# Entry and first layer of a two-layer fp32 backbone: clock products in a tile of their own, silu row copied in the last turn, two context dots from rows at hand, context projection behind the fourth conv

## The chip, the cores and the metric

The kernel runs on one core of one Trainium2 chip, as one launch. The metric is the device time in microseconds (us) of one execution; a result is the median of several runs. Five engines work side by side and wait for each other by semaphores: TensorE (PE: matmuls into PSUM), VectorE (DVE), ScalarE (ACT), GpSimd (POOL) and SyncE (SP), whose queue issues all loads here.

## The reference, cut to what matters

```python
def reference(x, c, ctx, c_ctx, ada_w, ada_b, ...):           # x (1,512,1024), ctx (1,256,1024), fp32
    for i in range(2):
        sh1, sc1, g1, sh2, sc2, g2 = ada(c, ada_w[i], ada_b[i])        # silu(c) @ ada_w + ada_b, in six parts
        csh1, csc1, ... = ada(c_ctx, ada_w[i], ada_b[i])
        h_l = rmsnorm(x, norm1_g[i]) * (1 + sc1) + sh1
        if i == 0:
            h_c = rmsnorm(ctx, norm1_g[i]) * (1 + csc1) + csh1
            p_lat, p_ctx = h_l @ w_in, h_c @ w_in                       # 384 q, 256 kv, 32 rotary key, 3 x 512 conv
            q, k, v = from rmsnorm(cq) @ w_uq, rmsnorm(ckv) @ w_ukv, norms and rotary   # latent and context
            a_l = softmax(q_l k_all^T) v_all                            # 8 heads, 512 queries, 768 keys
            b_gate, c_gate, u = split(p_lat[..., 672:], 3)
            s_l = b_gate * conv3(c_gate * u)                            # depthwise, width 3
            out_l = concat(a_l, s_l) @ w_o
        else:
            out_l = fourier(h_l) @ w_fourier
        x = x + g1 * out_l
        x = x + g2 * swiglu(rmsnorm(x, norm2_g[i]) * (1 + sc2) + sh2, ...)
    return x
```

The change lies in the first 150 us: the modulation of layer 0 (`ada`), the norm of x, the input projection of both streams and the conv.

## The kernel before

All activations are held transposed, with the 1024 features as eight tiles (k = 0..7) of 128 partitions, and the 512 latent or 256 context tokens along the row. Every operand of a matmul is split into a high and a low part (`h_hi`, `h_lo`, weights `...h`, `...l`), and `mm3` makes three matmuls of each product: high by high, high by low, low by high. A weight is loaded into one of six slots of the pool `rawp` (RAW = 6), cast by ScalarE into a high part and split by VectorE (`tensor_sub`, the name ending in `l`); high and low parts have three slots each, so a weight's cast waits until TensorE has finished with the weight three before. The rows of `ada_w` use the same six slots.

**Start.** ScalarE makes silu(c) and silu(c_ctx); TensorE spreads them over all partitions as rows, `sil0` in the PSUM tile cb0 (seen as `cb` in the trace) and `sil` in another, which ScalarE copies to `ccsil` at once. The row of silu(c) is wanted later in SBUF as `csil`, in two halves. VectorE, ScalarE and GpSimd square x, TensorE sums, VectorE makes the reciprocal root, and `first_rstd` transposes it into the first half of the PSUM tile `nxrb` (called `rb`). TensorE then runs `warm(WARM4, rb_tile)`, eight products of a matrix of ones (sixteen passes in the trace) whose result nobody reads and which keep its clock up; they are written to the second half of the same tile. ScalarE copies `rb` to SBUF as `rbs` for GpSimd; VectorE makes `xn` of the first tile, x times `rb`, straight from PSUM.

**The loop** goes over n = 0..7, k = ORDER[n] = 1, 2, 3, 4, 0, 5, 6, 7, with VectorE, ScalarE and TensorE in program order. `mod_dot(k, i)` is one VectorE instruction: a row of `ada_w` (128x1024) times `sil0` from PSUM, summed into one column of `mod` (the trace shows it as junk<-ada,cb with a DVE_READ_ACCUMULATOR behind it). In a turn ScalarE makes h_hi and nx of tile k, VectorE the first dot of the next tile, then h_lo of this one, then the second dot; ScalarE makes mod and amod from them and casts the next weight; TensorE takes 17 matmuls of the input projection into the tiles qkv0 to qkv2. GpSimd makes xn of the next tile. In turns 5 and 6 ScalarE also copies a half of `sil0` to `csil`.

**Behind the loop** the order is no longer written by hand: a scheduler places what the code names, instruction by instruction, so the order in the code sets priorities only. The code names two weight splits, the norms of cq and ckv, and then four calls of `conv(ct, side_work)`, each with three products of 24 matmuls: `ob`, `oc` and `ou`; after each product one more weight of the list `srcs` is loaded and split (`fetch`) and `side_work` is called. The side work of conv 0 and conv 1 is `ctx_work`: sixteen dots of rows of `ada_w` with `ccsil` (loads `adac`, written to `cmod`), the shift and scale of the context; then the context's norm (ncacc, ncst, ncrr, ncrb) and `norm_apply` (nct, hc_hi, hc_lo). `sq_q.mean` lets TensorE sum the squares of cq into `sqst`, which VectorE turns into `eps_q`; the slot of sqst is the one that `ob1` takes next. Between conv 2 and conv 3 stands the context projection `ckv` (69 matmuls), its norm (cc_hi, cc_lo, skcacc, skcst) and `rkv`. The side work of conv 2 and conv 3 is `g1w`, eight dots of the next modulation chunk with `csil`. Then follow `kpe` (the rotary key), four q tiles `qtok`, each with a rotary product on GpSimd that needs the table `rope_pack`, the k and v tiles and attention.

Of the kernel before, what the change touches and what calls it, by code (L numbers as in the profile page):

```python
# [58 lines left out]
WARM4 = 8  # L59
CTX_DOTS = 2  # L60
# [49 lines left out]
def backbone(ctx: ExitStack, tc: tile.TileContext, a, out):  # L110
    nc = Core(tc)
# [14 lines left out]
    def ps2(name):  # L126
        return ps["pool"].tile([P, 2, 512], F32, tag="s2", name=name, bufs=3)

    def ps1(name, bufs=2):
        return ps["pool"].tile([P, 512], F32, tag="b", name=name, bufs=bufs)  # L130
# [7 lines left out]
    def load(src, name, slots=None):  # L138
        t = slots(name) if slots else rawp.tile([P, src.shape[1]], F32, tag="raw", name=name)
        nc.sync.dma_start(out=t, in_=src)  # L140
        return t
# [22 lines left out]
    def step(it, n=1):  # L164
        for _ in range(n):
            next(it, None)
# [20 lines left out]
    cmod = const.tile([P, 16], F32, name="cmod")  # L187
# [11 lines left out]
    def dot(dst, w, vec):  # L199
        tc.keep_in_program_order(  # L200
            nc.vector.scalar_tensor_tensor(junk, w, 1.0, vec, op0=ALU.mult, op1=ALU.mult, accum_out=dst))
# [139 lines left out]
    def warm(n, on=None):  # L341

        o = (on or ps2("warm"))[:, 1]
        for i in range(n):
            nc.tensor.matmul(o[:, 0:P], ones, ones, start=True, stop=True)
# [4 lines left out]
    ccsil = p1.tile([P, D], F32, name="ccsil")  # L350
    warm(WARM)
    halves = [w.rearrange("p (two n) -> p two n", two=2) for w in (csil, ccsil)]
    sil0 = silu_rows(0)
    sil = silu_rows(1)
    warm(WARM2)
    rows = {}
# [62 lines left out]
    def first_rstd():  # L419

        st = ps2("nxst")[:, 0]
        sq = {}

        def square(k):
            sq[k] = early.tile([P, T], F32, tag="nsq", name=f"nxsq{k}", bufs=SQ_BUFS)
            xk = x[:, k, :]
            if k in SQ_DVE:
                nc.vector.tensor_mul(sq[k], xk, xk)
            elif k in SQ_POOL:
                tc.keep_in_program_order(nc.gpsimd.tensor_mul(sq[k], xk, xk))  # L430
            else:
                nc.scalar.activation(sq[k], xk, AF.Square)

        def col_sums(k, c):
            for t in range(4):
                nc.tensor.matmul(st[:, 4 * c + t:4 * c + t + 1], sq[k][:, t * P:(t + 1) * P], ones[:, 0:1], start=True, stop=True)

        for k in range(6):
            square(k)
            if k:  # L440
                nc.vector.tensor_add(sq[0], sq[0], sq[k])
        col_sums(0, 0)
        square(6)
        square(7)
        nc.vector.tensor_add(sq[7], sq[7], sq[6])
        col_sums(7, 1)
        mod_dot(order[0], 0)
        nc.scalar.copy(halves[1], sil)
        v, r = small("nxv", 4), small("nxr", 4)
        nc.vector.tensor_reduce(v, st[:, 0:8].rearrange("p (c t) -> p t c", c=2), op=ALU.add, axis=AX.X)  # L450
        nc.vector.tensor_scalar(v, v, 1.0 / D, EPS, op0=ALU.mult, op1=ALU.add)
        rsqrt(r, v, 4, "nxrs")
        rr = early.tile([P, 4, P], F32, name="nxrr")
        nc.vector.tensor_copy(rr, r.rearrange("p (t o) -> p t o", o=1).broadcast_to([P, 4, P]))
        o = ps2("nxrb")
        warm(WARM3, o)
        rb = o[:, 0]
        for t in range(4):
            nc.tensor.transpose(rb[:, t * P:(t + 1) * P], rr[:, t, :], ident)
        return rb, o  # L460

    order = ORDER
    mod_load(order[0])
# [2 lines left out]
    mod_load(order[1])  # L466
    mod_load(order[2])
    bias1 = p1.tile([P, KT], F32, name="bias1")
    rb, rb_tile = first_rstd()
    warm(WARM4, rb_tile)  # L470

    rbs = early.tile([P, T], F32, name="rbs")

    nc.vector.scalar_tensor_tensor(bias1, col(C_AB + 8, KT), 1.0, col(C_N1, KT), op0=ALU.add, op1=ALU.mult)
    mod_dot(order[0], 1)
    qkv_split(order[0])
    nc.scalar.copy(rbs, rb)
    nc.vector.tensor_mul(xn[:, order[0], :], x[:, order[0], :], rb)
    mod_finish(order[0])
    for fn in later:  # L480
# [7 lines left out]
    for n, k in enumerate(order):  # L488
        nxt, far, load_ = (order[n + i] if n + i < KT else None for i in (1, 2, 3))
        if load_ is not None:  # L490
            mod_load(load_)
        by_dve = nxt is not None and nxt >= NPE
        lo = hi_lo_affine(h_hi[:, k, :], h_lo[:, k, :], xn[:, k, :], amod0[:, k:k + 1], mod0[:, k:k + 1], T, f"nx{k}")
        if n in (5, 6):
            nc.scalar.copy(halves[0][:, n - 5], sil0[:, n - 5])
        if nxt is not None:
            tc.keep_in_program_order(nc.gpsimd.tensor_mul(xn[:, nxt, :], x[:, nxt, :], rbs))
        if by_dve:
            mod_dot(nxt, 0)
        lo()  # L500
        if n == 0 and XD == 2:
            nc.vector.tensor_mul(xn[:, nxt, :], x[:, nxt, :], rb)
        if by_dve:
            mod_dot(nxt, 1)
        if nxt is not None:
            mod_finish(nxt)
            qkv_split(nxt)
        by_pe = mod_pe(far) if far is not None and far < NPE else iter(())
        wh, wl = qw[k]
        r = (h_hi[:, k, :], h_lo[:, k, :])  # L510
        for i, (w, v) in enumerate(((wh, 0), (wl, 0), (wh, 1))):
            for m in range(5):
                nc.tensor.matmul((pq + pkv)[m], w[:, m * P:(m + 1) * P], r[v], start=(n == 0 and i == 0), stop=(n == 7 and i == 2))
                step(by_pe, 2)
            if i != 1:
                nc.tensor.matmul(ppe, wh[:, 640:704], r[v], start=(n == 0 and i == 0), stop=(n == 7 and i == 2))
# [18 lines left out]
        nc.vector.scalar_tensor_tensor(lo, src, g, f(hi), op0=ALU.mult, op1=ALU.subtract)  # L535

    srcs = [(f"wc{ct}_{w}", a["wconv"][ct, w]) for ct in range(3) for w in range(3)]
    srcs += [(f"wkvc{c}", a["wkvc"][c]) for c in range(3)]
    srcs += [(f"wc3_{w}", a["wconv"][3, w]) for w in range(3)]
    srcs += [(f"uq{k}", a["uq"][k]) for k in range(3)]  # L540
    stream, taken = [], []

# [70 lines left out]
    def ctx_work():  # L613
        for k in range(NPE, KT):
            for base in (0, 8):
                w = load(a["ada"][0, base + k], f"adac{base + k}")
                dot(cmod[:, base + k:base + k + 1], w, ccsil)
                yield
            nc.vector.tensor_add(pair_cols(cmod, k), pair_cols(cmod, k), pair_cols(cols[:, C_AB:C_AB + 16], k))
        scale_cols(camod, cmod[:, 8:16], col(C_N1, 8))  # L620
        rc = s_.rstd(0, L)
        yield
        norm_apply(p1, ctxT, rc, camod, cmod, hc_hi, hc_lo, 0, L, "nc")
        yield

    cw = ctx_work()
    conv(0, lambda: step(cw, CTX_DOTS))
    sq_q.mean(0, T, QL, eps_q)
    nc.vector.tensor_scalar_mul(eps_q, eps_q, EPS)
    conv(1, lambda: step(cw, CTX_DOTS))  # L630
# [2 lines left out]
    g1w = ada_chunk(0, 2)  # L633
    conv(2, lambda: step(g1w, 1))

    two, one_ = ps2("ckv01"), ps1("ckv2")
    ckv = [two[:, 0, 0:L], two[:, 1, 0:L], one_[0:ROPE, 0:L]]
    for c in range(3):
        w = weight()
# [10 lines left out]
    nc.scalar.copy(pe_f[0:32, T:T + L], ckv[2])  # L650
    sc_.mean(0, L, KVL, mkv[:, 4:6])
    rsqrt(rkv, mkv, 6, "rkv")
    conv(3, lambda: step(g1w, 2))
    step(g1w, 100)
    cv.release()
    p1.release()
# [780 lines left out]
    for t in range(4):  # L1437
        if t < 2:
            first(v1_ps[t], t, (3,))
            o = v1_ps[t]  # L1440
# [265 lines left out]
```

## Time and profile before

| | us |
|---|---|
| median of three runs | 1109.05 (1105.81 to 1110.4) |
| the profiled execution | 1111.21 |
| its span (first to last instruction) | 1109.4 |
| PE busy | 1072.6 (97%) |
| DVE busy | 862.5 (78%) |
| ACT busy | 533.0 (48%) |
| POOL busy | 134.1 (12%) |
| chain that ended last, by engine | PE 79%, DVE 11%, ACT 2%, issue 2%, DMA 1% |

The mean granted clock of TensorE is 0.983 of full speed. A busy TensorE is not TensorE at its peak, since matmuls are pipelined and their ends are modelled. In a row of a timeline the bracket gives the engine's idle time just before the instruction and what released it; a release can be a DMA that landed. Nearly every instruction has line L92, since a helper records it, so one goes by the names of tiles; the names leave out buffer numbers (`wc_0l` is the low part of the first weight of any of the four convs, `ob` the first product of any).

### The profile page before, as it was taken

To read this page: it belongs to the slowest core of one execution; us is meant where nothing else is said; L and a number is where in the kernel's file an instruction comes from. 1 tells how busy PE (TensorE), PEld (TensorE's weight loads), DVE (VectorE), ACT (ScalarE), POOL (GpSimd) and SP (SyncE) were. 2 spreads that over 40 slices of the span, in tenths; PEclk is the share of its full clock that TensorE was granted. 3 is DMA by queue.
4 is the path that set the end of the run, shared out by engine and by line. 5 is a ranking of instruction groups with operands and counts; after the bars stand their busy time and mean duration, and the time that the engine had idled before them with its cause. 6 is when DMAs were issued, how large, how long until landed. Compare 5 with 4: busy or idle time off the path is not lost.

```text
span 1109.4 us, 17136 instructions
## 1 busy us (share of the span) xinstructions
PE 1072.6 (97%) x6704; PEld 953.5 (86%) x6704; DVE 862.5 (78%) x1266; ACT 533.0 (48%) x842; POOL 134.1 (12%) x160
## 2 busy tenths in 40 slices
PE   8988998999999999999999999999999999999998
PEld 7667886888888898899989988987878899978997
DVE  5688868998789887889688989788895578745862
ACT  4553446898445452256415554363543155623550
POOL 1701138775000000000000000011000000000000
PEclk8998998999999999999999999898999999999999
DMA  7888540010661358643573573312425124431231
GB/s 251 289 300 267 171 154 24 23 56 27 223 226 58 120 183 267 208 152 117 188 230 132 172 256 134 95 58 82 147 72 163 51 88 140 134 96 67 76 95 67
DMA packets 45529, 156.96 MB, mean 141 GB/s; under 512 B 5252, under 2 KB 6276, under 8 KB 45320
## 3 DMA queue, kind: packets, MB, share of 16 engines
q1 hardware_dynamic: 45448, 155.87, 42.6%
q8 instruction: 52, 0.85, 0.3%
q14 instruction: 29, 0.24, 0.1%
HBM read 153.75 MB, written 2.10 MB: 140 GB/s over the span
## 4 chain that ended last, share of the span: by engine, by line
PE 79%; DVE 11%; ACT 2%; issue 2%; DMA 1%; POOL 0%; ACTq 0%; DVEq 0%; POOLq 0%
PE f L92 23%; PE s_a L92 13%; PE s_e L92 9%; PE s_f L92 4%; PE s_b L92 4%; PE s_ps L92 4%; PE o L92 3%; PE t_ps L92 2%; PE pv_ps L92 2%; PE ob L92 2%; PE z L92 2%; PE fo L92 2%; PE ou L92 2%; PE f_third L92 1%; DVE junk L92 1%
## 5 line engine op out<-in xcount | busy, mean ns | idle before, releaser
L92 DVE SCALAR_TENSOR_TENSOR junk<-ada,csil 128x1024 bf16<-128x1024 f32 x72 | 88.5, 1229 | 13.0 <-DMA ada<-in_ada 12.5
L92 DVE SCALAR_TENSOR_TENSOR x<-f,mod,x 128x512 f32<-128x512 f32 (+1 forms) x50 | 36.4, 728 | 66.1 <-PE f L92 66.0
L92 DVE TENSOR_TENSOR wu<-wu,wu 128x1024 f32<-128x1024 f32 x68 | 83.1, 1222 | 1.2
L92 POOL TENSOR_TENSOR w<-w,mod 128x1024 f32<-128x1024 f32 x4 | 7.9, 1974 | 478.0 <-DVE w_0l L92 460.1
L92 PE MATMUL s_a<-sh,w_s2h 128*128 128x256 f32 x136 | 38.5, 283 | 2.4 <-ACT s_b L92 2.4
L92 PE MATMUL s_a<-sh,w_s2l 128*128 128x256 f32 x136 | 38.5, 283 | 0.0
L92 PE MATMUL s_e<-sh,w_s1l 128*128 128x256 f32 x136 | 38.5, 283 | 0.0
L92 PE MATMUL s_e<-sh,w_s1h 128*128 128x256 f32 x136 | 38.3, 282 | 0.0
L92 PE MATMUL s_e<-sl,w_s1h 128*128 128x256 f32 x136 | 38.3, 282 | 0.0
L92 PE MATMUL s_a<-sh,w_s3l 128*128 128x256 f32 x136 | 38.3, 282 | 0.0
L92 PE MATMUL s_a<-sh,w_s3h 128*128 128x256 f32 x136 | 38.3, 282 | 0.0
L92 PE MATMUL s_a<-sl,w_s3h 128*128 128x256 f32 x136 | 38.2, 281 | 0.0
L92 PE MATMUL s_a<-sl,w_s2h 128*128 128x256 f32 x136 | 38.2, 281 | 0.0
L92 ACT CAST w_11h<-wu 128x1024 fp32r<-128x1024 f32 x17 | 17.8, 1049 | 41.1 <-PE f L92 18.0
L92 ACT CAST w_s2h<-wu 128x1024 fp32r<-128x1024 f32 x17 | 17.8, 1049 | 38.3 <-DVE wu L92 25.6
L92 DVE TENSOR_TENSOR w_22l<-wu,w_22h 128x1024 fp32r<-128x1024 f32 x17 | 20.8, 1225 | 19.2 <-ACT w_22h L92 19.2
L92 DVE TENSOR_TENSOR ptl<-t_ps,pth 128x384 fp32r<-128x384 f32 x62 | 31.4, 548 | 3.1 <-ACT pth L92 2.8
L92 POOL TENSOR_SCALAR p<-p,m 128x768 f32<-128x768 f32 x32 | 29.1, 910 | 25.1 <-DVE m L92 21.4
L92 DVE TENSOR_REDUCE m<-s_ps 128x1 f32<-128x768 f32 x32 | 30.3, 948 | 0.6 <-PE s_ps L92 0.5
L92 ACT CAST w_s1h<-wu 128x1024 fp32r<-128x1024 f32 x17 | 17.9, 1052 | 26.3 <-PE f L92 13.7
L92 ACT ACTIVATE p<-s_ps,m 128x768 f32<-128x768 f32 x32 | 29.2, 913 | 0.8 <-DVE m L92 0.8
L92 ACT CAST pth<-t_ps 128x384 fp32r<-128x384 f32 x62 | 26.7, 480 | 5.5 <-PE t_ps L92 5.1
(1016 smaller groups left out, 4174.5 us busy)
## 6 DMA issues: line engine op xcount, KB each, us to landing
ada<-in_ada SPq DMA_DIRECT2D x96, 512.0 KB, 4.4
wu<-in_wu SPq DMA_DIRECT2D x68, 512.0 KB, 3.8
w<-in_w SPq DMA_DIRECT2D x52, 512.0 KB, 4.2
adac<-in_ada SPq DMA_DIRECT2D x16, 512.0 KB, 4.8
wc<-in_wconv SPq DMA_DIRECT2D x12, 512.0 KB, 4.5
w<-in_w SPq DMA_DIRECT2D x16, 384.0 KB, 3.7
wo<-in_wo SPq DMA_DIRECT2D x8, 512.0 KB, 4.2
wf<-in_wf SPq DMA_DIRECT2D x8, 512.0 KB, 4.4
```

Of the source, the lines that this page charges most:

```text
L92: ins = fn(*args, **kw)
```

## The change

1. The clock products behind the transposes go to a tile of their own, `warm`, in place of the second half of `nxrb`.
2. ScalarE's copy `rbs` moves from before the first xn to behind h_hi and nx of turn 0.
3. Both halves of `csil` are copied in turn 7, in place of one each in turns 5 and 6.
4. In turn 7 VectorE makes the two context dots of tile 7 from the rows of `ada_w` that that turn's modulation has used (`rows[7]`), and `ctx_work` leaves tile 7 out: fourteen loads `adac` in place of sixteen.
5. Conv 0 steps the context dots once per weight in place of twice.
6. conv 3 is named before the context projection, and its weights before those of the projection in `srcs`.

```diff
         o = ps2("nxrb")
         warm(WARM3, o)
-        rb = o[:, 0]
+        rb = o[:, 0, :]
         for t in range(4):
             nc.tensor.transpose(rb[:, t * P:(t + 1) * P], rr[:, t, :], ident)
-        return rb, o
+        return rb
...
-    rb, rb_tile = first_rstd()
-    warm(WARM4, rb_tile)
+    rb = first_rstd()
+    warm(WARM4)
...
     qkv_split(order[0])
-    nc.scalar.copy(rbs, rb)
     nc.vector.tensor_mul(xn[:, order[0], :], x[:, order[0], :], rb)
...
-        if n in (5, 6):
-            nc.scalar.copy(halves[0][:, n - 5], sil0[:, n - 5])
+        if n == 0:
+            nc.scalar.copy(rbs, rb)
+        if n == 7:
+            for i in range(2):
+                nc.scalar.copy(halves[0][:, i], sil0[:, i])
...
         lo()
+        if n == 7:
+            for i, base in enumerate((0, 8)):
+                dot(cmod[:, base + k:base + k + 1], rows[k][i], ccsil)
...
     srcs = [(f"wc{ct}_{w}", a["wconv"][ct, w]) for ct in range(3) for w in range(3)]
+    srcs += [(f"wc3_{w}", a["wconv"][3, w]) for w in range(3)]
     srcs += [(f"wkvc{c}", a["wkvc"][c]) for c in range(3)]
-    srcs += [(f"wc3_{w}", a["wconv"][3, w]) for w in range(3)]
     srcs += [(f"uq{k}", a["uq"][k]) for k in range(3)]
...
             for base in (0, 8):
-                w = load(a["ada"][0, base + k], f"adac{base + k}")
-                dot(cmod[:, base + k:base + k + 1], w, ccsil)
-                yield
+                if k != order[7]:
+                    w = load(a["ada"][0, base + k], f"adac{base + k}")
+                    dot(cmod[:, base + k:base + k + 1], w, ccsil)
+                    yield
...
-    conv(0, lambda: step(cw, CTX_DOTS))
+    conv(0, lambda: step(cw, 1))
...
+    conv(3, lambda: step(g1w, 2))
     two, one_ = ps2("ckv01"), ps1("ckv2")
...
     rsqrt(rkv, mkv, 6, "rkv")
-    conv(3, lambda: step(g1w, 2))
     step(g1w, 100)
```

`warm` without a second argument takes a tile of the pool of pairs of PSUM banks, of which there are three; `warm` writes to its second half.

ScalarE at the start of the loop, before (wqkvh1 is the first weight's high part, nx1 and h_hi belong to turn 0):

```order
CAST wqkvh1_225<-wqkv1_143 128x672
COPY rbs_222<-nxrb_206 128x512
ACTIVATE mod_77<-mod_77,cols_68 128x1
ACTIVATE amod_79<-mod_77,bias1_159,cols_68 128x1
ACTIVATE h_hi_94<-xn_99,mod_77,amod_79 128x512
ACTIVATE nx1_243<-xn_99,mod_77,amod_79 128x512
```

and after:

```order
CAST wqkvh1_226<-wqkv1_143 128x672
ACTIVATE mod_77<-mod_77,cols_68 128x1
ACTIVATE amod_79<-mod_77,bias1_159,cols_68 128x1
ACTIVATE h_hi_94<-xn_99,mod_77,amod_79 128x512
ACTIVATE nx1_243<-xn_99,mod_77,amod_79 128x512
COPY rbs_223<-nxrb_206 128x512
```

The copy rbs stands four instructions later, behind the two that make turn 0's operand.

VectorE before eps_q, which releases ob1 (wc1_0l and wc1_1l are splits of conv 1's weights, a row with cmod_78<-adac is a context dot), before:

```order
TENSOR_TENSOR wc1_0l_657<-wc1_0_654,wc1_0h_656 128x1024
SCALAR_TENSOR_TENSOR junk_70,cmod_78<-adac3_758,ccsil_104 128x1024
SCALAR_TENSOR_TENSOR junk_70,cmod_78<-adac11_761,ccsil_104 128x1024
TENSOR_TENSOR cmod_78<-cmod_78,cols_68 128x2
TENSOR_TENSOR wc1_1l_696<-wc1_1_693,wc1_1h_695 128x1024
SCALAR_TENSOR_TENSOR junk_70,cmod_78<-adac4_795,ccsil_104 128x1024
SCALAR_TENSOR_TENSOR junk_70,cmod_78<-adac12_798,ccsil_104 128x1024
TENSOR_TENSOR cmod_78<-cmod_78,cols_68 128x2
TENSOR_SCALAR eps_q_518<-sqst0_717 128x4
```

and after:

```order
TENSOR_TENSOR wc1_0l_657<-wc1_0_654,wc1_0h_656 128x1024
SCALAR_TENSOR_TENSOR junk_70,cmod_78<-adac8_660,ccsil_104 128x1024
TENSOR_TENSOR cmod_78<-cmod_78,cols_68 128x2
SCALAR_TENSOR_TENSOR junk_70,cmod_78<-adac1_696,ccsil_104 128x1024
TENSOR_TENSOR wc1_1l_692<-wc1_1_689,wc1_1h_691 128x1024
TENSOR_SCALAR eps_q_521<-sqst0_710 128x4
```

Ahead of wc1_0l stood six context dots, and one does now; so ten dots of conv 0's and conv 1's work stood before eps_q, and three stand there now.

VectorE before wc2_2l, the low part that ou2 needs (z, y and mix are the conv's elementwise steps, ncv0 and ncrs0s belong to the context's norm), before:

```order
TENSOR_TENSOR wc2_1l_830<-wc2_1_827,wc2_1h_829 128x1024
TENSOR_TENSOR mix_84<-ob0_593,y0_710 128x512
TENSOR_TENSOR cmod_78<-cmod_78,cols_68 128x2
SCALAR_TENSOR_TENSOR camod_80<-cmod_78,cols_68 128x8
TENSOR_TENSOR z1_840<-ou1_725,cs1_801 128x512
TENSOR_SCALAR mkv_519<-skvst0_851 128x4
TENSOR_TENSOR wc2_2l_953<-wc2_2_950,wc2_2h_952 128x1024
```

and after:

```order
SCALAR_TENSOR_TENSOR junk_70,cmod_78<-adac12_850,ccsil_104 128x1024
SCALAR_TENSOR_TENSOR y1_837<-z1_833,cols_68,y1_837 128x512
TENSOR_TENSOR cmod_78<-cmod_78,cols_68 128x2
SCALAR_TENSOR_TENSOR junk_70,cmod_78<-adac5_854,ccsil_104 128x1024
TENSOR_TENSOR mix_84<-ob1_719,y1_837 128x512
SCALAR_TENSOR_TENSOR junk_70,cmod_78<-adac13_857,ccsil_104 128x1024
TENSOR_SCALAR ncv0_870<-ncst0_871 128x2
TENSOR_TENSOR cmod_78<-cmod_78,cols_68 128x2
SCALAR_TENSOR_TENSOR junk_70,cmod_78<-adac6_861,ccsil_104 128x1024
RECIPROCAL ncrs0s_876<-ncrs0s_876 128x2
TENSOR_TENSOR wc2_2l_950<-wc2_2_947,wc2_2h_949 128x1024
```

Before, all context dots were done ahead of wc2_1l; now they run up to wc2_2l, and one more (adac14) stands behind it.

## Rows read from the trace of the kernel before

**Rows 1.** Timeline of PE, 14 to 24 us: start, duration, instruction, [idle, releaser]

```profile
16.86 1.11 PE L92 MATMUL nxrb<-ident,nxrr 128*128 128x128 f32 x4 [1.19 <-DVE nxrr L92]
17.77 2.84 PE L92 MATMUL nxrb<-ones 128*128 128x128 f32 x16
22.91 1.55 PE L92 MATMUL qkv<-h_hi,wqkvh 128*128 128x512 f32 x3 [2.30 <-ACT h_hi L92]
```

**Rows 2.** The timeline of DVE, 14 to 34 us

```profile
17.94 0.08 DVE L92 DVE_READ_ACCUMULATOR junk<-ada,cb 128x1 f32 x1
21.26 0.69 DVE L92 TENSOR_TENSOR xn<-x,nxrb 128x512 f32<-128x512 f32 x1 [3.24 <-ACT rbs L92]
```

**Rows 3.** The timeline of DVE, 40 to 62 us

```profile
41.98 0.80 DVE L92 TENSOR_TENSOR h_lo<-nx,h_hi 128x512 fp32r<-128x512 f32 x1 [1.26 <-ACT nx L92]
...
46.91 1.22 DVE L92 SCALAR_TENSOR_TENSOR junk<-ada,cb 128x1024 bf16<-128x1024 f32 x1 [2.99 <-ACT csil L92]
...
48.06 0.69 DVE L92 TENSOR_TENSOR h_lo<-nx,h_hi 128x512 fp32r<-128x512 f32 x1
...
54.03 0.69 DVE L92 TENSOR_TENSOR h_lo<-nx,h_hi 128x512 fp32r<-128x512 f32 x1
...
58.38 0.78 DVE L92 TENSOR_TENSOR h_lo<-nx,h_hi 128x512 fp32r<-128x512 f32 x1 [2.52 <-ACT nx L92]
```

**Rows 4.** The timeline of PE, 60 to 96 us

```profile
62.17 0.39 PE L92 MATMUL ob<-h_hi,wc_0h 128*128 128x512 f32 x1
...
68.78 0.50 PE L92 MATMUL oc<-h_hi,wc_1h 128*128 128x512 f32 x1 [0.85 <-ACT skvacc L92]
...
80.08 0.95 PE L92 MATMUL sqst<-ones,sqacc 128*128 128x1 f32 x8
...
86.59 0.80 PE L92 MATMUL ob<-h_hi,wc_0h 128*128 128x512 f32 x1 [4.98 <-DVE eps_q L92]
...
94.42 0.40 PE L92 MATMUL oc<-h_hi,wc_1l 128*128 128x512 f32 x1
```

**Rows 5.** Windows: stretch, length, five engines, granted clock, DMA share, rate

```profile
87.00:95.00 8.00, 8.00 (x27) 6.31 (x27) 6.28 (x13) 1.86 (x4) 0.00 (x0) 0.73 0.89 299
95.00:105.00 10.00, 10.00 (x45) 7.97 (x43) 8.62 (x16) 4.52 (x8) 2.23 (x3) 1.00 0.92 311
```

**Rows 6.** The timeline of DVE, 80 to 106 us

```profile
85.04 1.22 DVE L92 SCALAR_TENSOR_TENSOR junk<-adac,ccsil 128x1024 bf16<-128x1024 f32 x1 [0.71 <-DMA adac<-in_ada]
...
86.39 0.15 DVE L92 TENSOR_SCALAR eps_q<-sqst 128x4 f32<-128x4 f32 x1
...
88.72 1.23 DVE L92 SCALAR_TENSOR_TENSOR junk<-adac,ccsil 128x1024 bf16<-128x1024 f32 x1 [1.97 <-DMA adac<-in_ada]
...
89.87 0.42 DVE L92 TENSOR_TENSOR ncacc<-ncacc,ncsq 128x256 f32<-128x256 f32 x1
90.20 1.22 DVE L92 TENSOR_TENSOR wc_2l<-wc,wc_2h 128x1024 fp32r<-128x1024 f32 x1
91.34 0.42 DVE L92 TENSOR_TENSOR ncacc<-ncacc,ncsq 128x256 f32<-128x256 f32 x1
...
104.31 0.69 DVE L92 TENSOR_TENSOR mix<-ob,y 128x512 f32<-128x512 f32 x1 [1.19 <-POOL z L92]
```

**Rows 7.** Chain of waits, 110 to 160 us: start, duration, group

```profile
112.74 5.60 PE ob L92 x24
...
123.71 8.15 PE ckv L92 x69
...
149.92 1.45 PE kpe_ps L92 x12
151.37 3.36 PE qtok L92 x18
...
156.55 0.40 DVE kr L92 x2
```

**Rows 8.** The page's DMA issues: group, KB each, us to landing

```profile
adac<-in_ada SPq DMA_DIRECT2D x16, 512.0 KB, 4.8
```

## The prediction

> **What bounds the kernel now.** TensorE is busy for 97% of the span, so the useful question is where it waits, and whether the edits touch those places. I read the instruction timeline of TensorE first, for the waits in brackets, then VectorE's timeline at the same times, to see what the releaser had been doing, then the granted clock by window, and last the chain of waits, for what carries a shift on to attention. In the first 62 us TensorE follows VectorE: the first projection matmul comes at 22.91 after 2.30 us of waiting for h_hi [rows 1], because VectorE's xn stood until 21.26, 3.24 us idle behind ScalarE's copy rbs [rows 2]. That copy reads the tile nxrb, into whose second half TensorE writes sixteen clock products from 17.77 to 20.61 [rows 1]. Then the loop is paced by VectorE and ScalarE: an undisturbed turn from h_lo to h_lo takes 4.35 us (54.03 to 58.38), but two turns take 6.08 and 5.97 us, each with a 2.99 us wait of a dot for ScalarE's csil copy [rows 3] (there are two such waits). From 62.17 TensorE is ahead and waits twice: 0.85 us before oc0, and 4.98 us before ob1, for eps_q [rows 4]. VectorE got to eps_q only at 86.39, since ten context dots and two weight splits stood in front of it, some late for their DMA [rows 6] (the dot at 85.04 is one of three such waits). After that gap the granted clock of the window 87 to 95 is 0.73 where the next has 1.00 [rows 5].
>
> **The change part by part.** *Clock products in their own tile.* xn now waits for the transposes alone, which end at 16.86 + 1.11 = 17.97; the dot before it is read out at 18.02 [rows 1, 2]. So xn starts at about 18.1 in place of 21.26: 3.2 us. The rbs copy, now behind h_hi and nx, ends near 18.1 + 4 x 0.69 = 20.9 (each step about as long as xn [rows 2]), so GpSimd, which waits for it, starts its first xn about as before, and that one is needed only a turn later; TensorE finishes the clock products at 20.6 and can start the projection at once. The loop is a chain through VectorE, so all 3.2 us carry to its end. Bounds: nothing (TensorE could be the later one if its first group runs at half rate), and 3.2; I take 3.2, since the wait behind an undisturbed turn is ScalarE's nx, not TensorE [rows 3], as at 58.38.
> The Trainium skill, page "PSUM — Partial Sum Buffer", section "PSUM bank collisions raise a hardware error", says that engines may use different banks side by side and clash only within one bank. The clock products already lay in another half of the tile, yet the copy waited for them [rows 1, 2], so the measurement says that here the wait goes by the whole tile. By the page too a separate tile leaves nothing to wait for, and the sum is the same.
>
> *csil copied in turn 7.* Without the copy the two dots of turns 5 and 6 start when VectorE is free, and both turns fall to the 4.35 us of the last: 6.08 + 5.97 - 2 x 4.35 = 3.35, of which I count 3.2, since most other turns are nearer 4.4. The copies now stand on ScalarE ahead of the cast of wc0_0, which has room. So the loop ends 6.4 us earlier and ob0, at 62.17 before, could start at 55.8.
>
> *Two context dots in turn 7, two loads dropped.* They cost VectorE 2 x 1.25 us right after h_lo, ahead of the split of wc0_0, whose result ob0's third matmul needs: 58.38 - 6.4 + 0.7 + 2.5 + 1.14 = 56.3, against 55.8 + 2 x 0.23 = 56.3. I put 0.2 us; the bound is 0 to 1. Two fewer loads of 512 KB relieve a busy queue and are counted at nothing.
>
> *Fewer dots in conv 0.* Before eps_q there were ten dots on VectorE, now there are three: 7 x 1.15 = 8.1 us less [rows 6], 88.72 to 89.87, and the three waits for loads go too. eps_q was late by 86.39 - 81.03, the end of sqst, = 5.4 us, so it is in time, and the gap before ob1 falls from 4.98 to some 0.2 us: 4.8 us. The wait before oc0 goes too (oc0 now takes the slot of qkv0, whose last reader on ScalarE is an earlier square than skvacc): 0.85. Without the gap, ob1 should run at full rate: it took 86.59 to 94.42, 7.83 us, where a conv product takes 5.60 [rows 4, 7]: 2.2 us.
>
> *Where those dots go.* Ten dots now stand between eps_q and the split of wc2_2, which ou2's third matmul needs. VectorE's work there, start to start from [rows 6]: ten dots at 1.15, four splits at 1.14, seven ncacc at 0.33, six 512-wide steps at 0.69 each, less their overlap (3.7 counted of 4.1), eight small ones (0.7): 22.8 us; plus 1.8 us in which the cast of wc2_0 waits for the end of ob1, and 1.2 for GpSimd's add before mix0, as at 104.31. That is 25.8 us. TensorE has ob1, 22 matmuls of oc1, ou1 and oc2 at 0.233 each (5.60, 5.13, 5.60, 5.60 [rows 7]), two column sums (0.8 and 0.5, from sqst's 0.95 [rows 4]), 0.2 for eps_q itself and two matmuls of ou2, 0.5: 23.9 us to the same point. So a **new wait of 1.9 us** in ou2, and 0.5 more at ncrb, whose norm stands behind two dots of the next chunk. Loss 2.4; bounds 0 (the loads early and the small steps hidden) and 5 (each of the last dots a little late).
>
> *Conv 3 ahead of the context projection.* The same matmuls in another order: ckv's 8.15 us and kpe's 1.45 us are paid in both [rows 7]. ob3 needs a slot freed by nct7: VectorE has fourteen steps of 256 columns before it (0.42 each, as ncacc), two splits and a dot, 9.3 us, TensorE has ob2 and twenty matmuls of oc3, 5.60 + 4.67 = 10.3 us: no wait. At the new border qtok0 needs uq2, whose slot ckv frees only at its end; its cast, 0.8, and split, 0.9 (three quarters of 1.14), with two short steps of ScalarE ahead, take some 2.4 us, and qtok0 has twelve matmuls first, two thirds of 3.36, 2.2 us [rows 7]. I take 0, bounds 0 to 1. kpe and skcst now run behind qtok0. The kr steps, which release GpSimd's rope and so the q and k chain up to attention, started 156.55 - 131.86 - 3 x 5.60 = 7.9 us behind the end of ckv, conv 3 left out; now they stand behind qtok0, two matmuls more, skcst and kpe, 3.4 + 0.3 + 0.6 + 1.45, and a copy of 0.3: 6.1, and five small steps of rkv, some 0.5, come among them. That is 1.3 us sooner. I count 0.5, because the rope load, which starts at the end of ckv as before, now has no conv 3 to cover it (on SP it also stands behind three row loads, and its products on GpSimd behind the add of conv 3); bounds -1.3 (gain) and +1.5 (kr waits for it).
>
> **Sum** against the profiled execution: -3.2 - 3.2 + 0.2 - 0.85 - 4.8 - 2.2 + 2.4 - 0.5 = -12.2 us. Its own time is 1111.2 us, which is 2.2 above the median of the three runs, 1109.05; so the changed kernel's profile should be near 1099.0 and its median near **1097 us**. What follows attention's start keeps its order and is bound by TensorE, so the shift should reach the end whole.
>
> **The rivals.** (1) *The clock falls at the new wait.* The 4.98 us gap was followed by slow matmuls [rows 5]; after the 0.85 us wait the 48 matmuls of oc0 and ou0 took 68.78 to 80.08, 0.235 each, full rate [rows 4]. 1.9 us lies between, and no row decides. It costs the same 2.2 us again: 1099.
> [...]
> (2) *The new tile doesn't free xn*: some other reader still holds it behind the clock products. Then 3.2 us stay: 1100. Against it: xn's only wait on TensorE is for the transposes. (3) *The border ckv to qtok0 loses instead of gaining*, by 2 to 3 us through uq2, skcst or the rope load: 1100. (4) *The moved dots wait for their loads.* This is the slower side. The ten dots behind eps_q share six load slots with weights that wait for TensorE. Before, one such dot stood 1.97 us for its DMA [rows 6]. If each of the ten did, ou2 would start 19.7 us later still: 1097 + 19.7 = 1117, slower. A mean of 0.65 us per dot brings it within 0.5%, and from 1.8 us it is slower by more. Against it: a load takes 4.8 us to land [rows 8], and by the new order each of these is issued when the third or fourth dot before it frees a slot, an estimated 5 us or more ahead; for it, that those three waits were there at all.
>
> **How the numbers follow.** Forecast as summed: 0.66, 1093 to 1100. Rival 1: 0.12; rival 2: 0.05; rival 3: 0.05; rival 4 in part (1104 to 1114): 0.08; in full: 0.04. A measurement of this kernel tells about 0.5% (5.5 us) from no change, so faster means below 1103.5. Faster is then the first four less a little for their tails, 0.87; same 0.09; slower 0.04. For 8 in 10 the range takes in rivals 1 to 3 and the unknown costs: no new wait gives 1094.5, with the border's whole 1.3 and csil's whole 3.35 1093.5, and the runs of the kernel before lie as far as 3.2 below their median, 1090; a new wait of 5 us with the clock's 2.2 gives 1102, and the border's worst 1104 to 1105. So 1090 to 1105.
>
> **What would show it.** Right: xn on VectorE near 18.1, no dot waiting for csil, h_lo of turn 7 near 52, ob0 near 56, ob1 right behind sqst near 74 with granted clock 1.00 between 75 and 95, a wait of about 2 us in ou2 near 98 for wc2_2l, ckv ending near 137, kr near 143. Wrong: xn still near 21; waits of VectorE for adac loads of a microsecond each between 75 and 100; a clock below 0.9 between 97 and 107; a gap between ckv and qtok1 above 1 us; or a shift at attention's start that the end doesn't keep.

## The result and the profile after

| us | before | after |
|---|---|---|
| median of four runs each, taken side by side | 1108.09 (1105.81 to 1110.4) | 1096.15 (1093.93 to 1097.64) |
| the profiled execution | 1111.21 | 1096.96 |
| its span | 1109.4 | 1095.2 |
| PE, DVE, ACT, POOL busy | 1072.6, 862.5, 533.0, 134.1 | 1066.9, 859.2, 533.3, 132.9 |

The ratio is 0.9891, with a 95% interval of 0.9862 to 0.9919: the changed kernel is 11.9 us faster. A second set of runs gave 1094.18 (six runs) against 1106.55 (eleven), ratio 0.9885 (0.9866 to 0.9904). Nearly the same work is done in both. PE is busy 5.7 us less, which fits the mean granted clock (0.983 before, 0.988 after), and the rest of the 14.2 us between the two spans is waiting.

The rows of the changed kernel follow in the order of rows 1 to 7. First TensorE's timeline from 14 to 24 us (start, duration, instruction, idle time before it and its releaser), which answers to [rows 1]:

```profile
17.22 1.11 PE L92 MATMUL nxrb<-ident,nxrr 128*128 128x128 f32 x4 [0.47 <-DVE nxrr L92]
18.13 3.01 PE L92 MATMUL warm<-ones 128*128 128x128 f32 x16
20.90 1.64 PE L92 MATMUL qkv<-h_hi,wqkvh 128*128 128x512 f32 x6
```

The clock products are now written to `warm`, and the projection follows them without a wait. VectorE's timeline, 14 to 102 us, answers to [rows 2, 3, 6]:

```profile
18.30 0.08 DVE L92 DVE_READ_ACCUMULATOR junk<-ada,cb 128x1 f32 x1
18.38 0.69 DVE L92 TENSOR_TENSOR xn<-x,nxrb 128x512 f32<-128x512 f32 x1
...
38.53 0.79 DVE L92 TENSOR_TENSOR h_lo<-nx,h_hi 128x512 fp32r<-128x512 f32 x1 [1.26 <-ACT nx L92]
...
42.99 0.78 DVE L92 TENSOR_TENSOR h_lo<-nx,h_hi 128x512 fp32r<-128x512 f32 x1 [1.26 <-ACT nx L92]
...
51.89 0.81 DVE L92 TENSOR_TENSOR h_lo<-nx,h_hi 128x512 fp32r<-128x512 f32 x1 [2.52 <-ACT nx L92]
...
73.78 0.16 DVE L92 TENSOR_SCALAR eps_q<-sqst 128x4 f32<-128x4 f32 x1 [1.92 <-PE sqst L92]
...
80.81 1.23 DVE L92 TENSOR_TENSOR wc_0l<-wc,wc_0h 128x1024 fp32r<-128x1024 f32 x1 [1.10 <-ACT wc_0h L92]
...
87.81 0.69 DVE L92 TENSOR_TENSOR mix<-ob,y 128x512 f32<-128x512 f32 x1 [1.48 <-POOL z L92]
...
96.98 0.69 DVE L92 TENSOR_TENSOR mix<-ob,y 128x512 f32<-128x512 f32 x1 [1.18 <-POOL y L92]
97.59 1.21 DVE L92 SCALAR_TENSOR_TENSOR junk<-adac,ccsil 128x1024 bf16<-128x1024 f32 x1
...
98.92 1.22 DVE L92 SCALAR_TENSOR_TENSOR junk<-adac,ccsil 128x1024 bf16<-128x1024 f32 x1
...
100.14 1.20 DVE L92 TENSOR_TENSOR wc_2l<-wc,wc_2h 128x1024 fp32r<-128x1024 f32 x1
```

xn starts right behind the dot; all turns of the loop take 4.3 to 4.5 us; eps_q is ready as soon as TensorE has sqst, so that now VectorE waits (1.92 us); and between eps_q and wc_2l no dot waits for its load, but one split waits for its cast (1.10 us) and two mix steps wait for GpSimd. TensorE's timeline, 50 to 103 us, answers to [rows 4]:

```profile
55.71 0.39 PE L92 MATMUL ob<-h_hi,wc_0h 128*128 128x512 f32 x1
...
61.60 0.39 PE L92 MATMUL oc<-h_hi,wc_1h 128*128 128x512 f32 x1
...
72.80 0.95 PE L92 MATMUL sqst<-ones,sqacc 128*128 128x1 f32 x8
73.61 0.49 PE L92 MATMUL oc<-h_hi,wc_1h 128*128 128x512 f32 x1
...
74.16 0.39 PE L92 MATMUL ob<-h_hi,wc_0h 128*128 128x512 f32 x1
...
97.80 0.51 PE L92 MATMUL ou<-h_hi,wc_2h 128*128 128x512 f32 x1 [0.20 <-ACT wc_2h L92]
...
101.40 0.50 PE L92 MATMUL ou<-h_hi,wc_2l 128*128 128x512 f32 x1 [2.87 <-DVE wc_2l L92]
```

The waits before oc0 and ob1 are gone. The new wait is in ou2: 2.87 us for the split that VectorE starts at 100.14, and 0.20 us two matmuls earlier. The windows (stretch, length, busy time and count of PE, PEld, DVE, ACT and POOL, granted clock, DMA share, GB/s) answer to [rows 5]:

```profile
74.00:80.00 6.00, 6.00 (x27) 4.86 (x26) 5.50 (x12) 1.73 (x5) 0.00 (x0) 1.00 0.84 270
87.00:95.00 8.00, 8.00 (x42) 6.72 (x41) 7.16 (x14) 1.58 (x3) 1.12 (x4) 1.00 0.69 241
100.00:110.00 10.00, 8.60 (x31) 6.86 (x32) 8.10 (x21) 2.85 (x4) 0.00 (x0) 0.83 0.92 335
```

The low clock behind ob1's gap is gone, and there is a new one behind ou2's wait. The chain of waits from 95 to 168 us (start, duration, group) answers to [rows 7]:

```profile
101.40 6.94 PE ou L92 x22
108.34 0.22 PE ncrb L92 x2
108.56 5.60 PE ob L92 x24
114.16 4.67 PE oc L92 x20
118.83 5.60 PE ob L92 x24
124.43 0.93 PE oc L92 x4
125.36 5.60 PE ou L92 x24
130.96 8.48 PE ckv L92 x72
139.44 3.69 PE qtok L92 x20
...
145.34 0.36 DVE kr L92
```

From 108.34 to 143 nothing interrupts TensorE: ob3 and qtok0 come without a wait. The 22 matmuls of ou2 took 6.94 us where at full rate they take 22 x 0.233 = 5.13.

### The profile page after: what moved, and what is told of

Same layout as the page of the kernel before. It is cut to its first block, busy times and chain, and to the rows that moved or that the text cites. A ratio compares the mean times of both kernels' runs of the same rounds, so it can differ in the third digit from the quotient of the medians.

```text
span 1095.2 us, 17132 instructions
## 1 busy us (share of the span) xinstructions
PE 1066.9 (97%) x6704; PEld 950.4 (87%) x6704; DVE 859.2 (78%) x1266; ACT 533.3 (49%) x842; POOL 132.9 (12%) x160
## 4 chain that ended last, share of the span: by engine, by line
PE 80%; DVE 12%; ACT 3%; issue 3%; DMA 1%; POOL 1%; SPq 0%; DVEq 0%; ACTq 0%; POOLq 0%
PE f L92 24%; PE s_a L92 13%; PE s_e L92 9%; PE s_f L92 4%; PE s_b L92 4%; PE s_ps L92 4%; PE o L92 3%; PE t_ps L92 2%; PE pv_ps L92 2%; PE ob L92 2%; DVE junk L92 2%; PE ou L92 2%; PE fo L92 2%; PE f_third L92 1%; PE f_first L92 1%
## 5 line engine op out<-in xcount | busy, mean ns | idle before, releaser
L92 ACT CAST w_s1h<-wu 128x1024 fp32r<-128x1024 f32 x17 | 17.9, 1051 | 26.2 <-PE f L92 13.7
```

The costliest lines, as they stand in the source:

```text
L92: ins = fn(*args, **kw)
```

## The experiments

Each kernel is made from one of the two kernels by the edit shown. The first eight have one run each, so they are read at landmarks of the trace rather than by their times: the first xn, h_lo of turn 7, ob0, oc0, GpSimd's first rope step (`xq`), and attention's first transpose of k. Kernels with the same start reach xn between 17.9 and 19.5 us, so a difference below a microsecond in a landmark says nothing by itself; where it matters, the landmark is counted from xn.

| kernel | xn | h_lo 7 | ob0 | oc0 | xq | k | time |
|---|---|---|---|---|---|---|---|
| before | 21.26 | 58.38 | 62.17 | 68.78 | 158.25 | 177.46 | 1108.09 |
| after | 18.38 | 51.89 | 55.71 | 61.60 | 147.38 | 167.10 | 1096.15 |
| e1, clock products back in nxrb | 21.27 | 54.79 | 58.61 | 67.83 | 155.28 | 175.00 | 1104.97 |
| e2, rbs copied before xn | 18.98 | 53.07 | 56.89 | 62.78 | 149.72 | 169.42 | 1099.83 |
| e3, csil copied in turns 5 and 6 | 17.92 | 54.47 | 58.26 | 63.85 | 149.62 | 169.33 | 1099.85 |
| e4, conv 0 steps two dots | 19.15 | 52.69 | 56.51 | 62.40 | 157.43 | 177.14 | 1107.79 |
| e5, no dots of tile 7 in turn 7 | 17.91 | 51.45 | 55.26 | 60.86 | 149.55 | 168.59 | 1096.50 |
| e6, conv 3 behind the projection | 18.66 | 52.20 | 56.03 | 61.91 | 149.82 | 169.02 | 1099.68 |
| e7, before + conv 0 steps one | 21.27 | 58.38 | 62.17 | 68.79 | 159.30 | 178.50 | 1104.45 |
| e8, before + the three loop edits | 18.65 | 52.17 | 55.99 | 61.59 | 158.23 | 177.40 | 1104.27 |

**e1: the clock products back in the other half of nxrb**, the copy rbs left behind nx.

```diff
-    rb = first_rstd()
-    warm(WARM4)
+    rb, rb_tile = first_rstd()
+    warm(WARM4, rb_tile)
```

> The changed kernel with one thing undone: the eight clock products stand in the second half of nxrb again; the rbs copy stays behind nx of turn 0. Theory (the wait goes by the whole tile, and the loop is one chain): xn on VectorE waits for the end of the clock products, near 21.2 us in place of 18.4; h_lo of turn 7 comes 2.6 to 2.9 us later, near 54.6; the first transpose of k_tok in attention (167.1 in the changed kernel) near 169.9. Rival (different halves are different banks, nothing waits): xn stays near 18.4 and nothing moves. Second rival (TensorE takes up the shift later): xn late, but k_tok's transpose within 0.5 us of 167.1.

VectorE's timeline of e1, 14 to 24 us:

```profile
21.27 0.69 DVE L92 TENSOR_TENSOR xn<-x,nxrb 128x512 f32<-128x512 f32 x1 [3.40 <-PE nxrb L92]
```

and its TensorE's, 55 to 69 us:

```profile
67.83 0.50 PE L92 MATMUL oc<-h_hi,wc_1h 128*128 128x512 f32 x1 [3.17 <-ACT skvacc L92]
```

xn waits again, 3.40 us, with no copy ahead of it: the tile was the cause, and the loop ends 2.9 us later, as expected. The rest was not: k comes 7.9 us later where 2.8 had been expected. The wait before oc0 came back as 3.17 us, and in the window behind it (68 to 74 us) the granted clock was 0.72. The tile `warm` is one more draw from the pool of PSUM pairs; without it the tiles behind take other slots, and oc0 gets one whose last reader is the late skvacc. That reading of the slots is argued from the order of the tiles in the code and the name of the releaser. So the new tile did two things: it freed xn, and it spared oc0 a wait.

**e2: the copy rbs back before the first xn**, the tile of its own kept.

```diff
+    nc.scalar.copy(rbs, rb)
     nc.vector.tensor_mul(xn[:, order[0], :], x[:, order[0], :], rb)
...
-        if n == 0:
-            nc.scalar.copy(rbs, rb)
```

> The changed kernel with one thing undone: ScalarE's copy rbs stands before the first xn again; the clock products keep their own tile. Theory (two readers of one tile go one after the other): xn starts behind the copy, near 19.1 in place of 18.4, and everything up to attention 0.6 to 0.7 us later. Rival (the move of the copy is the part that matters): xn near 21, all 3 us lost. Rival (readers don't wait for each other): xn stays at 18.4.

xn comes at 18.98 behind a wait of 0.61 us for rbs, and from xn to h_lo of turn 7 it is 34.09 us against 33.51. So the place of the copy is worth about 0.6 us at xn and 0.6 more in the loop; the tile carries the 2.9. k comes 2.3 us later, where 0.6 to 0.7 was expected: 1.1 us of it arises behind the loop. ou2 waits as long as in the changed kernel there (0.84 and 2.24 us), but the window from 100 to 110 us reads 0.66 in place of 0.83.

**e3: csil copied in turns 5 and 6.**

```diff
-        if n == 7:
-            for i in range(2):
-                nc.scalar.copy(halves[0][:, i], sil0[:, i])
+        if n in (5, 6):
+            nc.scalar.copy(halves[0][:, n - 5], sil0[:, n - 5])
```

> The changed kernel with one thing undone: the halves of csil are copied in turns 5 and 6 again. Theory: two waits of about 3.0 us of VectorE's dots for ScalarE come back, the two turns take 6.0 us each, h_lo of turn 7 comes near 55.1 in place of 51.9, and k_tok's transpose near 170.3 (167.1). Rival (a load or ScalarE holds these turns anyway): h_lo of turn 7 less than 1 us later.

VectorE's timeline of e3, 36 to 56 us:

```profile
43.01 1.22 DVE L92 SCALAR_TENSOR_TENSOR junk<-ada,cb 128x1024 bf16<-128x1024 f32 x1 [2.99 <-ACT csil L92]
...
48.98 1.22 DVE L92 SCALAR_TENSOR_TENSOR junk<-ada,cb 128x1024 bf16<-128x1024 f32 x1 [2.99 <-ACT csil L92]
```

Both waits of [rows 3] are back, to the hundredth. From xn to h_lo of turn 7 it is 36.55 us against 33.51: 3.0 us. k comes 2.2 us later (2.7 counted from xn), where 3.2 was expected.

**e8: the kernel before with the three loop edits alone** (own tile, rbs, csil), and **e4: the changed kernel with conv 0 stepping two dots** again.

```diff
-    conv(0, lambda: step(cw, 1))
+    conv(0, lambda: step(cw, CTX_DOTS))
```

> The kernel before with the loop's parts alone: clock products in their own tile, rbs behind nx, csil in turn 7; context dots, their steps and the place of conv 3 as before. Theory: h_lo of turn 7 near 51.9, ob0 near 55.9, no wait before oc0; but 13 context dots now stand before eps_q, so TensorE waits 6 to 8 us before ob1 and its clock falls behind that wait; k_tok's transpose near 172 (177.5 before, 167.1 with the whole change). Rival (the loop's gain is swallowed by the wait for eps_q): near 177. Rival (the loop is all there is): near 168.

> The changed kernel with conv 0 stepping two context dots per weight again. Theory (dots in front of eps_q are what TensorE waits for): fourteen dots stand before eps_q where five do, so the gap before ob1 comes back, 6 to 9 us, with a low clock behind it; the wait in ou2 goes (2.9 us and its low clock); k_tok's transpose 3 to 6 us later than 167.1. Rival (the DMA loads, not the dots, made eps_q late, and two loads fewer cure that): gap under 2 us.

TensorE's timeline of e8, 70 to 92 us:

```profile
86.02 0.79 PE L92 MATMUL ob<-h_hi,wc_0h 128*128 128x512 f32 x1 [11.70 <-DVE eps_q L92]
```

VectorE's timeline of e8, 64 to 88 us:

```profile
72.26 1.22 DVE L92 SCALAR_TENSOR_TENSOR junk<-adac,ccsil 128x1024 bf16<-128x1024 f32 x1 [2.08 <-DMA adac<-in_ada]
...
74.56 1.23 DVE L92 SCALAR_TENSOR_TENSOR junk<-adac,ccsil 128x1024 bf16<-128x1024 f32 x1 [1.07 <-DMA adac<-in_ada]
...
79.48 1.23 DVE L92 SCALAR_TENSOR_TENSOR junk<-adac,ccsil 128x1024 bf16<-128x1024 f32 x1 [1.21 <-DMA adac<-in_ada]
...
85.81 0.16 DVE L92 TENSOR_SCALAR eps_q<-sqst 128x4 f32<-128x4 f32 x1
```

The loop of e8 ends 6.2 us earlier than before, and eps_q still comes at 85.81 (before: 86.39). VectorE uses up its lead in waits for loads of ada rows: the three shown and 0.91 and 0.26 behind them. So e8's rival held, the gain swallowed by the wait for eps_q, and not its theory. e4 shows the same from the other side: 11.37 us in front of ob1, and k 10.0 us later than in the changed kernel, where 3 to 6 had been expected. So what set eps_q in the kernel before was the arrival of the rows, more than VectorE's own time for the dots; whether the rows are late for the rate of the loads or for the slots that the loads wait for was not tried. The trace of e8 points to the slots. Among the waits of the queue of loads, 50 to 90 us (engine, what it waited for, us in total, times, longest), the largest is for dots, which free the slots:

```profile
SPq L140 <- DVE junk L92: 11.0, 9, 2.1
```

and the chain that ends in eps_q goes from a dot to a load of 5.73 us, a dot, a load of 3.57, a dot and a load of 3.62.

The whole gain of the loop was worth nothing as long as those rows stood ahead of eps_q.

**e7: the kernel before with conv 0 stepping one dot**, nothing else (the diff of e4 read upwards).

> The kernel before with one edit: conv 0 steps one context dot per weight. Theory: loop as before (h_lo of turn 7 near 58.4), the 4.98 us gap before ob1 and the low clock behind it go (7.0 us), and a wait of 3 to 5 us with a low clock comes up in ou2, because twelve dots now stand between eps_q and the split of wc2_2; k_tok's transpose near 176 (177.5 before). Rival (the moved dots fit beside TensorE's work): near 170.5. Rival (they cost as much as they free, or more): 177.5 or later.

TensorE's timeline of e7, 104 to 114 us:

```profile
108.46 0.60 PE L92 MATMUL ou<-h_hi,wc_2h 128*128 128x512 f32 x1 [3.56 <-ACT wc_2h L92]
...
111.32 0.80 PE L92 MATMUL ou<-h_hi,wc_2l 128*128 128x512 f32 x1 [1.83 <-DVE wc_2l L92]
```

The gap before ob1 goes, but with TensorE that much earlier and the loop as late as before, ou2 waits 3.56 us for wc_2h and 1.83 for wc_2l, with a granted clock of 0.66 from 108 to 118; k comes 1.0 us later than before, as its second rival had it. So neither half of the change gains anything at attention (177.40, 178.50, before 177.46), and both together, with the two smaller edits, gain 10.4 us.

**e5: the dots of tile 7 back among the loads**, sixteen of them.

```diff
-        if n == 7:
-            for i, base in enumerate((0, 8)):
-                dot(cmod[:, base + k:base + k + 1], rows[k][i], ccsil)
...
-                if k != order[7]:
-                    w = load(a["ada"][0, base + k], f"adac{base + k}")
+                w = load(a["ada"][0, base + k], f"adac{base + k}")
```

> The changed kernel without the two dots of tile 7 in the last turn; that tile's rows are loaded again (sixteen loads adac). Theory: nothing changes up to eps_q, but twelve dots, not ten, stand between eps_q and the split of wc2_2, so the wait in ou2 grows from 2.9 to about 5 us; k_tok's transpose 2 to 3 us later than 167.1. Rival (these dots lie in VectorE's idle time): within 0.7 us of 167.1.

TensorE's timeline of e5, 95 to 105 us:

```profile
100.83 0.79 PE L92 MATMUL ou<-h_hi,wc_2h 128*128 128x512 f32 x1 [3.97 <-ACT wc_2h L92]
103.28 0.79 PE L92 MATMUL ou<-h_hi,wc_2l 128*128 128x512 f32 x1 [1.23 <-DVE wc_2l L92]
```

ou2 waits 5.2 us in all, against 3.07. The two dots stand on VectorE again, and the split starts at 102.00 in place of 100.14; the load of wc_2 lands later too, so that its cast starts at 99.73 in place of 96.70. k is 1.5 us later, or 2.0 counted from xn.

**e6: conv 3 behind the projection.**

```diff
-    srcs += [(f"wc3_{w}", a["wconv"][3, w]) for w in range(3)]
     srcs += [(f"wkvc{c}", a["wkvc"][c]) for c in range(3)]
+    srcs += [(f"wc3_{w}", a["wconv"][3, w]) for w in range(3)]
...
-    conv(3, lambda: step(g1w, 2))
...
     rsqrt(rkv, mkv, 6, "rkv")
+    conv(3, lambda: step(g1w, 2))
```

> The changed kernel with conv 3 behind the context projection again, its weights too. Theory: kr and the q chain start 0.5 to 1.3 us later relative to TensorE's work, and TensorE waits a little for hc or skcst; k_tok's transpose 0.3 to 1.5 us later than 167.1. Rival (the order is what frees conv 2 and conv 3 from waiting): 3 us or more later. Rival (the new border costs): earlier than 166.6.

k comes 1.9 us later (1.6 counted from xn), with a wait of 1.10 us in oc3 for its split: the new order is worth a little more than was expected.

**e9 to e12: less work in front of ou2's split.** Six timed runs each; e9 is the changed kernel again. e10 moves the last context dots into conv 2, and the next chunk's dots to conv 3:

```diff
-    step(cw, 100)
     g1w = ada_chunk(0, 2)
-    conv(2, lambda: step(g1w, 1))
+    conv(2, lambda: step(cw, 2))
+    step(cw, 100)
```

e11 steps one dot in conv 1 and three in conv 2; e12 is e10 with three dots of the next chunk per weight in conv 3, so that none are left behind it.

> The changed kernel as it is, beside the next two variants. Every theory: the wait of some 2.9 us in ou2 for wc_2l near 101 us, the transpose of the context's k near 167, a time near 1096 us and about 11 to 12 us under the kernel before on the same chip. If a lower granted clock behind that wait comes and goes by chance, this run's window 100 to 110 can read above 0.83.

> Only the side work of conv 2 is changed: the last context dots and the norm of the context stay unfinished in front of conv 2 and go on between its products (two steps each), and the dots of the next chunk move to conv 3. So VectorE has six context dots between eps_q and the split that ou2 waits for, in place of ten. Theory (the wait is VectorE's queue of dots): 4 x 1.15 = 4.6 us less in front of that split, the wait of 2.87 us and its low clock (1.8 us) go, the transpose of k comes near 162 to 163, the time is 3.5 to 5 us under the changed kernel. Rival (the same work is only late at the next place): a wait of 1 to 3 us in ob3, ckv or its successors for hc_lo, the gain is under 1.5 us.

> As the variant before it, with conv 1 stepping one dot for each weight in place of two and conv 2 three in place of two: fewer still in front of the split, more behind it. Theory: no wait in ou2 either, so the same time as that variant within 1 us unless the dots left behind make hc_lo late; in that case a wait in ob3 or in ckv of 1 to 3 us, and a time that much longer. Rival: VectorE is late in any split, and both variants gain under 1.5 us.

> The variant e10 with one number changed: conv 3 steps three dots of the next chunk for each weight in place of two, so that its last two dots stand inside conv 3 and no longer among the steps kr. In e10 TensorE reached qtok0 5.6 us earlier than in the changed kernel, and the transpose of k only 2.2. Theory: these two dots (2.4 us on VectorE between the kr steps, which GpSimd's rope waits for) take part of what is missing, the other part being the rope table, whose load lands too late for it to follow; then xq on GpSimd starts near 143.5 in place of 145.85, the transpose of k comes near 162.0 in place of 164.3, and the time is some 2 us under e10's, 1092. Rival: the two dots make the splits of the weights for ckv or qtok0 late by as much; then ckv or qtok0 shows a wait of 1 to 2.4 us and the transpose of k stays near 164.

| | xn | qtok0 | xq | k | median | ratio to before, 95% |
|---|---|---|---|---|---|---|
| e9 | 18.40 | 139.34 | 147.44 | 166.46 | 1094.18 | 0.9885 (0.9866 to 0.9904) |
| e10 | 17.93 | 133.73 | 145.85 | 164.29 | 1094.19 | 0.9888 (0.9870 to 0.9907) |
| e11 | 19.48 | 135.28 | 147.16 | 165.63 | 1093.72 | 0.9885 (0.9860 to 0.9909) |
| e12 | 18.53 | split | 145.55 | 164.33 | 1092.84 | 0.9877 (0.9852 to 0.9902) |

(In e12 the first two matmuls of qtok0 stand inside ckv, so its start is not comparable.)

A window of e10, columns as above:

```profile
100.00:110.00 10.00, 10.00 (x46) 8.14 (x46) 7.80 (x15) 3.77 (x6) 0.00 (x0) 1.00 0.84 295
```

VectorE's queue in front of the split was the cause of ou2's wait: with four dots fewer, and with steps of the context's norm and mix1 with its wait for GpSimd behind the split too, the wait and the low clock are gone, and TensorE reaches qtok0 5.6 us earlier. What the dots alone are worth was not tried. But k comes only 2.2 us earlier and the time does not move; by its ratio none of the three can be told from e9. The gain is lost in front of attention, as VectorE's timeline of e10, 134 to 146 us, shows:

```profile
141.79 0.22 DVE L92 TENSOR_TENSOR kr<-kpe,rope_pack 128x64 f32<-128x64 f32 x1 [1.28 <-POOL rope_pack L92]
...
142.34 1.22 DVE L92 SCALAR_TENSOR_TENSOR junk<-ada,csil 128x1024 bf16<-128x1024 f32 x1
...
143.69 1.22 DVE L92 SCALAR_TENSOR_TENSOR junk<-ada,csil 128x1024 bf16<-128x1024 f32 x1
```

kr waits for the rope table, and two leftover dots stand between its steps. The chain of waits of e10 names the table's load ahead of it:

```profile
134.82 4.89 DMA rope_pack<-in_rope
139.85 1.92 POOL rope_pack L92 x4
```

In all kernels of both tables the transpose of k follows GpSimd's first xq by 18.4 to 19.7 us, and xq is released by kr: attention's start hangs on the rope's start, and TensorE's lead at qtok0 counts only as far as kr follows it. In e12 those dots are out of the way, and the rival of its expectation held. TensorE's timeline of e12, 133 to 140 us:

```profile
138.01 0.44 PE L92 MATMUL qtok<-uq1l,cq_hi 128*128 128x384 f32 x1 [0.96 <-DVE uq1l L92]
```

The two dots, now ahead of the splits, delay qtok0's weights, with them kpe, and so kr: xq comes at 145.55, 0.3 us earlier than in e10, and k at the same time. VectorE's work in front of attention only changes places.

## Why the prediction was right, step by step

The forecast was 1097 us; the median is 1096.15, and the profiled run, foreseen near 1099.0, took 1096.96. Single steps were off in both directions, and that they cancel so well is in part luck, as the sum below shows:

| step | said | measured |
|---|---|---|
| first xn | 18.1, so -3.2 | 18.38, -2.9; e1 gives 2.9 back |
| csil | -3.2 | xn to h_lo 7: 37.12 to 33.51, -3.6; e3 gives 3.0 back, e2 0.6 (the copy rbs) |
| ob0, third matmul | +0.2 | h_lo 7 to ob0 3.79 and 3.82; third matmul 0.2 late |
| wait before oc0 | -0.85 | ob0 to oc0 6.61 and 5.89, -0.7 |
| gap before ob1, low clock behind | -4.8 and -2.2 | -5.15 (from sqst's start to ob1 6.51 and 1.36) and -2.2 |
| new wait in ou2 | +1.9 | 3.07 |
| wait at ncrb | +0.5 | none |
| low clock behind the new wait (rival 1) | +2.2, in 12 of 100 | +1.8, it came |
| border to q and k, up to k's transpose | -0.5 | -0.8 |

**The start of the loop** went as worked out. A row explains the csil term: e3's two dots wait 2.99 us for ScalarE's copy, though both only read the row `cb`. The Trainium skill, page "PSUM — Partial Sum Buffer", section "PSUM bank collisions raise a hardware error", says that reads of one bank by two engines must be kept apart just as writes must; the trace agrees, 2.99 us twice in e3 and none in the changed kernel. Where the page goes by the bank, e1 shows a wait by the tile: the products lay in the other half of a pair of banks, and xn waited 3.40 us. The prediction gave the move of rbs nothing of its own; e2 shows 0.6 us in the loop.

**The gap before ob1** was sized nearly rightly (4.8 us said, 5.15 measured), but the reason given for it was only a part. The prediction set it down to VectorE's time for seven dots and named the waits for loads beside them. e8 and e4 show that the loads, with what they wait for, were the bound: with VectorE 6.2 us ahead, eps_q moved by 0.6. Had the change had only its loop part, the prediction's way of adding would have promised 6.4 us, and e8 shows 0.1 at attention. The terms of the sum could be added only because the edit that takes rows from in front of eps_q was among them.

**The new wait in ou2** is the mis-sized term: 1.9 was said, 2.87 measured and 0.20 ahead of it. The count of dots, splits and small steps gave 25.8 us from eps_q to the end of wc_2l; the trace has 73.94 to 101.34, 27.4. What it left out is a second wait for GpSimd: it counted one add before mix0 (1.2 us, measured 1.48), and mix1, which now stands ahead of wc_2l too, waits 1.18 us for another. VectorE's own steps took 23.6 us for the 22.8 counted, and the wait for the cast of wc2_0 1.10 for 1.8. TensorE needed 24.6 us to the same point for the 23.9 counted, so that less than the 1.6 us shows as a wait. The half microsecond at ncrb, on the other side, did not come, since ou2 kept TensorE busy until 108.34.

**The clock** fell behind this wait; the forecast had left that to rival 1, which came. Rows of these runs now lie between its two cases. In ou2 TensorE waited twice, two matmuls apart, for 0.84 and 2.24 us (e2), 0.83 and 2.24 (e3), 0.57 and 2.51 (e9), 0.24 and 2.82 (e1), 0.20 and 2.87 (after), or once for 3.32 (e6). Each time a window of ten microseconds there (100 to 110, in e1 108 to 118) reads 0.66 to 0.83, so a part of it ran at the lower level, 1.2 GHz. Behind e12's 0.52 and 0.96 us and e6's 1.10 in oc3 the clock stays at 1.00. The size of the wait alone does not decide it: behind the wait for k_tok at attention, 3.18 us before and 3.16 us in e7, the next 6 us (columns as above) read

```profile
177.46:183.46 6.00, 6.00 (x16) 4.82 (x17) 5.49 (x16) 2.25 (x6) 6.00 (x16) 0.50 0.00 1
178.50:184.50 6.00, 6.00 (x29) 4.84 (x30) 5.57 (x16) 3.82 (x10) 6.00 (x16) 1.00 0.00 1
```

the first in the kernel before, the second in e7. The Trainium skill, page "TensorE: Matmul & The Clock Gate", section "HAM oscillation — how this bites in real kernels", says that waits between batches can make the next batch start slow; behind the 2.87 us the trace agrees, with 22 matmuls in 6.94 us in place of 5.13. The waits of that section's own case are longer than this one, and for how short a wait can do it these rows decide.

**The sum at attention** is -10.4 us at the transpose of k where -12.2 was said (the rows of the table add up to -10.5, with the third matmul's 0.2 inside the row of oc0). The low clock and the larger wait in ou2 cost 2.5 more than was counted, and the loop, the gap and the border gave 0.8 more. The rest of the median's 11.9 us arises behind that point, where the forecast had expected nothing; in the profiled pair it is 3.9 us. Part of that is the clock: from 177 to 200 us before it reads 0.86, in the same stretch after (167 to 190) 0.93, and from the transpose of k to the next one of k it is 8.63 us before and 7.42 after. The change is not shown to be the cause: the first 6 us of that stretch read 0.72 to 0.74 in e8, which has the loop's part alone, and in most of the others, 0.55 in e11 and 1.00 in e7, where the same way takes 5.86 us. What makes up the rest behind attention's start stays open. So the terms of the sum are seen one by one in the traces, but that its end lies within a microsecond of the median is luck in part: 1.8 us missing at attention were made good behind it. Two of the signs named for being wrong came: a clock below 0.9 between 97 and 107 us (0.83), and a shift at attention's start that is not that of the end (-10.4 and -11.9 us).

**The slower rival**, dots that wait for their loads, did not come: no dot behind eps_q waits. e8 shows that it was near: ahead of eps_q dots wait for their loads five times there.

## What to carry to other kernels

When an engine is late at one place, give it a lead in one experiment before counting its instructions: if the late step does not move, the bound is what the engine itself waits for, here the arrival of rows, and the gains of earlier edits are swallowed until that is taken out of the way. Two edits that gain nothing alone (k at 177.40 and 178.50 us) can gain 10 us together, so a single edit's null result is not proof against it. And a load or product moved past a wait needs its own line in the sum for every engine that the moved steps themselves wait for, GpSimd's adds above all.

## What the runs showed of the hardware that was not expected

- Two engines that only read one PSUM row are kept apart: 2.99 us for a dot that waits for a copy of the row it reads (e3, twice).
- Waits of 3.1 to 3.3 us in ou2, whole or in two parts two matmuls apart, were each time followed by a stretch at the lower clock; it cost 1.8 us behind 3.07 us in the changed kernel. A wait of 3.16 us at attention (e7) was followed by full clock, and one of 3.18 us in the kernel before by 6 us at the lower level, so the length of the wait does not settle it.
- With one tile less in a pool of PSUM slots another product, far from the place where it is written, waited 3.17 us (e1); that the slots were dealt out otherwise is argued, as said there.
